# A two-layer diffusion backbone on one core: the first attention projection's weights are split beside the latents, and four pooling steps stand ahead of it

## The chip, the cores and the metric

The kernel runs on one core of one Trainium2 chip. The metric is the device time of one execution in microseconds (us), as the median of several runs. The core's engines each work through their own list of instructions in order: PE (TensorE, matrix products), DVE (VectorE), ACT (ScalarE), POOL (GpSimd) and SP (SyncE, which here only issues transfers from HBM).

## What is computed

Two layers over 256 latent tokens and 256 context tokens of width 2048; layer 0 is the one that the change touches. Cut to what matters:

```python
def even_mixer(hx, hc, w_in, q_norm, w_uq, kv_norm, w_ukv, w_pool, pool_scale, w_out, cos, sin, ctx_out):
    px = hx @ w_in                      # 512 query latents, 256 key/value latents, 64 rotary keys, 1024 pooling
    pc = hc @ w_in
    qn, qr = mla_queries(px, q_norm, w_uq)      # rmsnorm(query latents) @ w_uq, 8 heads
    kn, kr, v = mla_keys(px, kv_norm, w_ukv)    # rmsnorm(kv latents) @ w_ukv
    ckn, ckr, cv = mla_keys(pc, kv_norm, w_ukv)
    qr, kr = apply_rope(qr, cos, sin), apply_rope(kr, cos, sin)
    attn_x = latent_attention(qn, qr, concat(ckn, kn), concat(ckr, kr), concat(cv, v))
    pool_x = multiscale_pool(px[..., MLA_IN:], w_pool, pool_scale)   # 4 centred windows, then a 256x256 matrix each
    return concat(attn_x, pool_x) @ w_out
```

Around it stand adaptive norms (each scale and shift is a product of the conditioning vector with a 2048 x 2048 matrix), a squared-ReLU MLP of width 8192 in both layers, and a Fourier mixer in layer 1. All of it is float32.

## The kernel before

Activations lie transposed, features on partitions. A float32 product is made of three products of rounded halves: a weight tile `W` is loaded (`load`, 1 MB at most, six buffers), ACT rounds it into `H` (`split`, L135), DVE computes the rest `L = W - H` (L136), and PE multiplies H and L with the activations, H first. `H` and `L` have six buffers each. The second half of an activation is made in the same way (`split_pair`, `split_act`).

The adaptive vectors of layer 0 that the first stage doesn't need (`mod_vector`, 48 tiles of 1 MB) are not PE's work: DVE multiplies each tile with the conditioning vector and sums it, one SCALAR_TENSOR_TENSOR per tile (L103). `load` issues them: 1.75 of them for each weight tile in the mixer (`pace`), and all 48 must be summed before the norm that follows the mixer. They use the same six W buffers.

The mixer is two generators. `attention` squares the latents, makes their inverse norms (`var`, `rb`), scales them into kvh/kvl and ql, and then for each of four pairs of heads calls `project` (keys' part kn from w_ukv, the rotary query qr and the other query part qn from w_uq, values v), `scores` (with the softmax), `turned` (transposes of the probabilities) and `values`. `pooling` goes through the second half of the pooling input: four tiles of w_pl, each split in two halves, a step of 12 matmuls into `pu` for each half (steps 1 to 8 below; tiles 1 to 4), then `pl` (the windows, from the constants `band`), `po` (w_pool), and the pooled half of the output matrix w_oe. `weave` drives attention and, wherever it yields n, lets pooling take n steps. So the written order of the weave is the order of PE and of SP's transfers (both are in a manual schedule). The order of ACT and DVE is made by a scheduler when the kernel is built, and is fixed from then on.

Before the change, pooling takes one step after the squares, one after the first sums, and two after the latents; then `project(0)` loads and splits its two tiles. A blank step stands between step 8 and `pl`.

Of the kernel before, what the change touches and what calls it, by code (L numbers as in the profile page):

```python
# [43 lines left out]
def hybrid_dit(ctx: ExitStack, tc: tile.TileContext, xT, ctxT, c2, cb_in, vecs, wmod_s, wmod0, wmod1,  # L44
               w_kq, w_pl, w_uq, w_ukv, w_pool, w_oe, w_oo, w1, w2,
               rope, band, ident_in, sel_in, dftc, dftn, out):
    nc = tc.nc
# [14 lines left out]
    def funit(name="fu"):  # L62
        return ap.tile([P, 512], F32, name=name, tag="a")
# [13 lines left out]
    def half(b, i):  # L77
        return b[:, i * T:(i + 1) * T]
# [14 lines left out]
    def mod_step():  # L93
        l, which, norm, j, src = todo.pop(0)
        w = wp.tile([P, 2048], F32, name="W", tag="W")
        nc.sync.dma_start(w, src)
        late.append((w, l, which, norm, j))

    def mod_sums():

        while late:
            w, l, which, norm, j = late.pop(0)
            nc.vector.scalar_tensor_tensor(w, w, 1.0, cb, ALU.mult, ALU.mult,  # L103
                                           accum_out=mods[l][:, which, j:j + 1])
            if j == NB - 1:
                whole.add((l, which))
                v = mods[l][:, which]
                b = V_BM[l] + which * NB
                nc.vector.tensor_tensor(v, v, vec[:, b:b + NB], ALU.add)
                if norm is not None:  # L110
                    scales(mods[l], which, norm)
# [9 lines left out]
    def load(src, n=2048):  # L121
        mod_sums()
        w = wp.tile([P, 2048], F32, name="W", tag="W")
        nc.sync.dma_start(w[:, :n], src)
        pace[1] += pace[0]
        while pace[1] >= 1 and todo:
            pace[1] -= 1
            mod_step()
        return w

    def split(w, lo, n, nn):

        h = hp.tile([P, 1024], F32R, name="H", tag="H")
        l = hp.tile([P, 1024], F32R, name="L", tag="L")
        nc.scalar.copy(h[:, :n], w[:, lo:lo + n])  # L135
        nc.vector.tensor_tensor(l[:, :n], w[:, lo:lo + n], h.bitcast(F32)[:, :n], ALU.subtract)  # L136
        return [(h[:, i:i + nn], l[:, i:i + nn]) for i in range(0, n, nn)]

    def split_act(u, src, n=T):
        nc.scalar.copy(u[:, :n], src)  # L140
        nc.vector.tensor_tensor(u[:, n:2 * n], src, u.bitcast(F32)[:, :n], ALU.subtract)  # L141

    def split_pair(h, l, src):
        nc.scalar.copy(h, src)
        nc.vector.tensor_tensor(l, src, h.bitcast(F32), ALU.subtract)
# [195 lines left out]
    def column(i):  # L341
        return vec[:, i:i + 1]
# [153 lines left out]
    ropet = funit("ropet")  # L496
    nc.sync.dma_start(ropet.rearrange("p (a b) -> p a b", b=T), rope)
    bandt = [funit(f"band{i}") for i in range(4)]
    for i in range(4):
        nc.sync.dma_start(bandt[i], band[:, i])  # L500

    mod_vector(0, 2)
    mod_vector(0, 4, V_N2[0])
# [31 lines left out]
    def pooling():  # L535

        ut = [[funit("ut") for hf in range(2)] for tb in range(2)]
        for tb in range(2):
            nc.scalar.copy(ut[tb][0], pu0[tb])
        us = [bank(f"pu{tb}") for tb in range(2)]  # L540
        for kt in range(4):
            w = load(w_pl[1, kt])
            for i in range(2):
                for n, (h, l) in enumerate(split(w, 1024 * i, 1024, 512)):
                    by_token(us, 4 * kt + 2 * i + n, h, l)
                yield
        for tb in range(2):
            nc.scalar.copy(ut[tb][1], us[tb])
        yield
        pooled = []  # L550
        for g in range(4):
            ps = bank("pl")
            for j in range(2):
                fs = slice((g % 2) * T + j * P, (g % 2) * T + (j + 1) * P)
                for tb in range(2):
                    mm(half(ps, j), ut[tb][g // 2][:, fs], half(bandt[g], tb), j == 0 and tb == 0, j == 1 and tb == 1)
            pooled.append(funit("pl"))
            nc.scalar.copy(pooled[g], ps)
            if g % 2:
                yield  # L560
        w = load(w_pool)
        for g in range(4):
            ps = bank("po")
            for j in range(2):
                plain(half(ps, j), [w[:, k * 256:(k + 1) * 256] for k in (2 * g, 2 * g + 1)], j,
                      [half(pooled[g], 0), half(pooled[g], 1)], j == 0, j == 1)
            for j in range(2):
                u = unit("mx")
                sc, o = column(V_PS + 2 * g + j), half(ps, j)
                nc.scalar.mul(u[:, :T], o, sc)  # L570
                nc.vector.scalar_tensor_tensor(u[:, T:], o, sc, u.bitcast(F32)[:, :T], ALU.mult, ALU.subtract)
                mixed.append(u)
            if g % 2:
                yield
        for ng in range(4):
            yield from linear([((w_oe[ng, kt],), 4 * kt - 8) for kt in (2, 3)], mixed,
                              residual(0, 2, None, True)(ng), 4, True)
# [4 lines left out]
    def rotary(s):  # L582

        r = scr("rot")
        nc.vector.stream_shuffle(r, s, list(range(16, 32)) + list(range(16)))
        nc.vector.tensor_tensor(s, s, half(ropet, 0), ALU.mult)
        nc.vector.tensor_tensor(r, r, half(ropet, 1), ALU.mult)
        nc.vector.tensor_tensor(s, s, r, ALU.add)

    def attention():  # L590
        squares = []
        for b in ka[:2] + qa:
# [16 lines left out]
        for j in range(2):  # L609
            f = funit("kvf")  # L610
            nc.vector.scalar_tensor_tensor(f, ka[j], column(V_KN + j), rk, ALU.mult, ALU.mult)
            kvh.append(unit("kvh"))
            kvl.append(unit("kvl"))
            split_pair(kvh[j], kvl[j], f)
        for j in range(4):
            f = scr("ql")
            nc.vector.scalar_tensor_tensor(f, half(qa[j // 2], j % 2), column(V_QN + j), rq,
                                           ALU.mult, ALU.mult)
            ql.append(unit("qls"))
            split_act(ql[j], f)  # L620
        kr = funit("kr")
        nc.scalar.copy(kr, ka[2])
        rotary(half(kr, 1))
        krh, krl = unit("krh"), unit("krl")
        split_pair(krh, krl, kr)
        yield 2

        def project(pr):

            w = load(w_ukv[pr], 1024)  # L630
            wkv = split(w, 0, 1024, 512)
            kn, vt = [], []
            for j in range(2):
                js = slice(j * P, (j + 1) * P)
                ps = bank("kn")
                for k in range(2):
                    h, l = wkv[k]
                    mm(ps, h[:, js], kvh[k], k == 0, False)
                    mm(ps, h[:, js], kvl[k], False, False)
                    mm(ps, l[:, js], kvh[k], False, k == 1)  # L640
                kn.append((unit("knh"), unit("knl")))
                split_pair(*kn[j], ps)
            w = load(w_uq[pr], 1536)
            wuq = split(w, 0, 768, 384) + split(w, 768, 768, 384)
            ps = bank("qr")
            narrow(half(ps, 0), wuq, 2, ql, True, True)
            f = scr("qr")
            nc.scalar.copy(f, half(ps, 0))
            rotary(f)

            qr = (unit("qrh"), unit("qrl"))
            for j in range(2):
                nc.scalar.mul(half(qr[0], j), f, own[:, j:j + 1])
                nc.vector.scalar_tensor_tensor(half(qr[1], j), f, own[:, j:j + 1], half(qr[0], j).bitcast(F32),
                                               ALU.mult, ALU.subtract)
            ps = bank("qn")
            for j in range(2):
                narrow(half(ps, j), wuq, j, ql, j == 0, j == 1)
            qn = (unit("qnh"), unit("qnl"))
            split_pair(*qn, ps)  # L660
            for tb in range(2):
                ps = bank("v")
                for i in range(2):
                    ts = slice((2 * tb + i) * P, (2 * tb + i + 1) * P)
                    for k in range(2):
                        h, l = wkv[k]
                        mm(half(ps, i), kvh[k][:, ts], h[:, T:], k == 0 and i == 0, False)
                        mm(half(ps, i), kvl[k][:, ts], h[:, T:], False, False)
                        mm(half(ps, i), kvh[k][:, ts], l[:, T:], False, k == 1 and i == 1)
                vt.append(funit("v"))  # L670
                nc.scalar.copy(vt[tb], ps)
            return qn, qr, kn, vt
# [43 lines left out]
            attn.append(a)  # L716

        pair = project(0)
        yield 1
        p = scores((pair, 0))  # L720
        yield 2
# [272 lines left out]
```

## Time and profile before

| | us |
|---|---|
| median of 3 runs | 1979.73 |
| lowest, highest | 1978.56, 1980.13 |
| profiled execution, its own time | 1980.76 |
| its span in the trace | 1979.0 |
| PE busy / DVE busy / ACT busy | 1928.8 / 1455.6 / 1008.4 |
| mean busy share of the DMA engines by q1 | 72.9% |

A busy PE is not a PE at its peak: what counts is where it stands still and at what clock it runs. In the page's strip of 40 slices PE is at 90% or more in every slice but the first ones and the last; slice 4 of the granted clock reads 8 where nearly all others read 9. The places where PE waits are read from its instructions in order of time.

### The profile page before, as it was taken

Reading aid. Unit: us, or ns where it says so; the run is one execution under the profiler, and the core shown is the slowest. Engines: PE = TensorE matmul, PEld = TensorE weight load, DVE = VectorE, ACT = ScalarE, POOL = GpSimd, SP = SyncE. Lnnn points to the kernel's source line nnn. Section 1 sums busy time; section 2 is a strip of 40 time slices with the busy share of each in tenths; the row PEclk is TensorE's granted clock in tenths of the full one; section 3 lists DMA queues with packets and bytes.
Section 4 is the critical chain, followed back from the end, with each engine's and each line's share of the span. In section 5 each row is a group of like instructions: output and inputs, shape, how many; then the busy total and the mean of one; then the engine's idle time right before and its main releaser. Section 6 shows DMA issues by size and latency. Waiting matters only on the chain.

```text
span 1979.0 us, 29675 instructions
## 1 busy us (share of the span) xinstructions
PE 1928.8 (97%) x11886; PEld 1708.6 (86%) x11886; DVE 1455.6 (74%) x2042; ACT 1008.4 (51%) x1655; POOL 1.2 (0%) x13
## 2 busy tenths in 40 slices
PE   5998999999999999999999999999999999999997
PEld 4786899988888888888888989888888888888887
DVE  4548999998888888888888577897555555555564
ACT  3344654455545645554554454555455446544653
POOL 0000000000000000000000000000000000000000
PEclk9998999999999999999999999999999999999999
DMA  9997899879888888888998347597555555555541
GB/s 376 395 394 263 322 347 354 331 269 380 315 334 339 333 312 346 321 333 305 329 333 309 125 156 269 191 391 297 186 194 189 192 191 184 199 179 186 189 171 43
DMA packets 77466, 537.72 MB, mean 272 GB/s; under 512 B 8848, under 2 KB 9104, under 8 KB 14480
## 3 DMA queue, kind: packets, MB, share of 16 engines
q1 hardware_dynamic: 77328, 535.82, 72.9%
q8 instruction: 93, 1.52, 0.3%
q14 instruction: 45, 0.37, 0.1%
HBM read 533.69 MB, written 2.10 MB: 271 GB/s over the span
## 4 chain that ended last, share of the span: by engine, by line
PE 92%; DVE 5%; DMA 1%; issue 1%; ACT 1%; SPq 0%; DVEq 0%; ACTq 0%
PE mm L81 80%; PE ka L81 2%; DVE W L103 2%; PE mrow L81 1%; PE pu L81 1%; PE f L81 1%; PE qa L81 1%; DVE L L136 1%; PE sc L81 1%; DMA W<-in_wmod_s 1%; PE pv L81 1%; PE p L81 1%; PE var L81 0%; PE wk L81 0%; PE pl L81 0%
## 5 line engine op out<-in xcount | busy, mean ns | idle before, releaser
L136 DVE TENSOR_TENSOR L<-W,H 128x1024 fp32r<-128x1024 f32 (+1 forms) x620 | 736.3, 1213 | 266.2 <-ACT H L135 162.8
L135 ACT CAST H<-W 128x1024 fp32r<-128x1024 f32 (+1 forms) x620 | 628.8, 1042 | 526.6 <-PE mm L81 409.1
L81 PE MATMUL mm<-hid,H 128*128 128x512 f32 (+1 forms) x2176 | 509.8, 378 | 0.0
L81 PE MATMUL mm<-h,H 128*128 128x512 f32 x2048 | 495.1, 391 | 0.0
L81 PEld LDWEIGHTS mm<-hid,H 128*128 128x128 f32 x2176 | 390.9, 189 | 66.6
L81 PEld LDWEIGHTS mm<-h,H 128*128 128x128 f32 x2048 | 374.3, 188 | 72.0 <-DVE h L302 1.0
L103 DVE SCALAR_TENSOR_TENSOR W<-W,cb 128x2048 f32<-128x2048 f32 x160 | 364.7, 2283 | 0.2 <-DMA W<-in_wmod 0.2
L81 PE MATMUL mm<-hid,L 128*128 128x256 f32 x2048 | 290.0, 283 | 0.0
L81 PEld LDWEIGHTS mm<-hid,L 128*128 128x128 f32 x2048 | 274.7, 191 | 11.7
L81 PEld LDWEIGHTS mm<-h,L 128*128 128x128 f32 x2048 | 266.8, 191 | 12.5
L81 PE MATMUL mm<-h,L 128*128 128x256 f32 x2048 | 270.6, 283 | 0.0
L522 DVE SCALAR_TENSOR_TENSOR x<-mm,mods,x 128x256 f32<-128x256 f32 x176 | 81.2, 479 | 90.0 <-ACT rt L521 72.7
L758 DVE TENSOR_TENSOR g<-mm,b 128x256 f32<-128x256 f32 x128 | 53.7, 420 | 49.4 <-ACT b L757 48.6
L521 ACT ACTIVATE rt<-mm,mods 128x256 f32<-128x256 f32 x132 | 58.8, 470 | 61.0 <-PE mm L81 60.9
L757 ACT COPY b<-mm 128x256 f32<-128x256 f32 x128 | 45.8, 358 | 64.5 <-PE mm L81 64.5
L760 ACT ACTIVATE rl<-g 128x256 f32<-128x256 f32 x128 | 53.4, 417 | 47.2 <-DVE g L758 45.8
L81 PE MATMUL mm<-fr,H 128*128 128x512 f32 (+1 forms) x320 | 69.5, 348 | 0.0
L81 PEld LDWEIGHTS mm<-fr,H 128*128 128x128 f32 x320 | 55.1, 190 | 6.7
L761 ACT ACTIVATE hd<-rl 128x256 f32<-128x256 f32 x128 | 53.3, 417 | 3.0
L141 DVE TENSOR_TENSOR hid<-hd,hid 128x256 fp32r<-128x256 f32 x128 | 53.6, 419 | 0.5 <-ACT hid L140 0.5
L524 DVE TENSOR_TENSOR x<-x,rt 128x256 f32<-128x256 f32 x132 | 52.4, 418 | 1.1
L140 ACT CAST hid<-hd 128x256 fp32r<-128x256 f32 x128 | 52.2, 408 | 1.0
(224 smaller groups left out, 1558.8 us busy)
## 6 DMA issues: line engine op xcount, KB each, us to landing
W<-in_w SPq DMA_DIRECT2D x256, 1024.0 KB, 4.9
W<-in_wmod SPq DMA_DIRECT2D x160, 1024.0 KB, 6.1
W<-in_wmod_s SPq DMA_DIRECT2D x32, 1024.0 KB, 9.7
W<-in_w_oe SPq DMA_DIRECT2D x16, 1024.0 KB, 6.9
W<-in_w_oo SPq DMA_DIRECT2D x16, 1024.0 KB, 4.9
W<-in_w_pl SPq DMA_DIRECT2D x8, 1024.0 KB, 8.8
W<-in_w_kq SPq DMA_DIRECT2D x8, 896.0 KB, 9.4
W<-in_w_uq SPq DMA_DIRECT2D x4, 768.0 KB, 4.6
```

The source lines that it names most:

```text
L81: nc.tensor.matmul(o, l, r, start=start, stop=stop, skip_group_check=True)
L103: nc.vector.scalar_tensor_tensor(w, w, 1.0, cb, ALU.mult, ALU.mult, accum_out=mods[l][:, which, j:j + 1])
L135: nc.scalar.copy(h[:, :n], w[:, lo:lo + n])
L136: nc.vector.tensor_tensor(l[:, :n], w[:, lo:lo + n], h.bitcast(F32)[:, :n], ALU.subtract)
L140: nc.scalar.copy(u[:, :n], src)
L141: nc.vector.tensor_tensor(u[:, n:2 * n], src, u.bitcast(F32)[:, :n], ALU.subtract)
L521: nc.scalar.mul(t, half(ps, 1), g)
L522: nc.vector.scalar_tensor_tensor(x[:, i], ps[:, :T], g, x[:, i], ALU.mult, ALU.add)
L524: nc.vector.tensor_tensor(x[:, i], x[:, i], t, ALU.add)
L758: nc.vector.tensor_tensor(s, half(ps, 0), b, ALU.add)
L760: nc.scalar.activation(r, s, AF.Relu)
L761: nc.scalar.square(f, r)
```

## The change

`project(0)` no longer loads its weights itself. Its w_ukv tile is loaded and split when the key latents are scaled, its w_uq tile when the query latents are (`ready`); later pairs load as before. Attention yields 4 instead of 2 ahead of `project(0)`, so pooling steps 3 to 6 stand there instead of 3 and 4. The rotation of the keys' rotary part, and its split, are written behind `project(0)`. The four loads of the band constants, which stood ahead of the mixer, follow the weights of pooling tiles 1 to 4 one by one. The blank pooling step is gone.

```diff
-    for i in range(4):
-        nc.sync.dma_start(bandt[i], band[:, i])
@@ pooling()
                     by_token(us, 4 * kt + 2 * i + n, h, l)
                 yield
+            nc.sync.dma_start(bandt[kt], band[:, kt])
         for tb in range(2):
             nc.scalar.copy(ut[tb][1], us[tb])
-        yield
         pooled = []
@@
+    def key_weights(pr):
+        return split(load(w_ukv[pr], 1024), 0, 1024, 512)
+
+    def query_weights(pr):
+        w = load(w_uq[pr], 1536)
+        return split(w, 0, 768, 384) + split(w, 768, 768, 384)
@@ attention()
             split_pair(kvh[j], kvl[j], f)
+        ready = [key_weights(0)]
         for j in range(4):
@@
             split_act(ql[j], f)
+        ready.append(query_weights(0))
         kr = funit("kr")
         nc.scalar.copy(kr, ka[2])
-        rotary(half(kr, 1))
         krh, krl = unit("krh"), unit("krl")
-        split_pair(krh, krl, kr)
-        yield 2
+        yield 4
         def project(pr):
-            w = load(w_ukv[pr], 1024)
-            wkv = split(w, 0, 1024, 512)
+            wkv = ready.pop(0) if ready else key_weights(pr)
@@
-            w = load(w_uq[pr], 1536)
-            wuq = split(w, 0, 768, 384) + split(w, 768, 768, 384)
+            wuq = ready.pop(0) if ready else query_weights(pr)
@@
         pair = project(0)
+        rotary(half(kr, 1))
+        split_pair(krh, krl, kr)
         yield 1
```

DVE's list right behind the norm of the latents, before. The first row is the second half of pooling tile 2 (for step 4), the last one w_ukv of pair 0; kvf, kvl, ql and qls are the scaled latents and their splits:

```order
L136 TENSOR_TENSOR L<-W,H 128x1024
L611 SCALAR_TENSOR_TENSOR kvf<-ka_113,vec,rk 128x512
L617 SCALAR_TENSOR_TENSOR ql<-qa_111,vec,rq 128x256 x2
L617 SCALAR_TENSOR_TENSOR ql<-qa_112,vec,rq 128x256
L145 TENSOR_TENSOR kvl<-kvf,kvh 128x512
L611 SCALAR_TENSOR_TENSOR kvf<-ka_114,vec,rk 128x512
L617 SCALAR_TENSOR_TENSOR ql<-qa_112,vec,rq 128x256
L103 SCALAR_TENSOR_TENSOR W,mods_102<-W,cb 128x2048
L145 TENSOR_TENSOR kvl<-kvf,kvh 128x512
L141 TENSOR_TENSOR qls<-ql,qls 128x256 x4
L585 STREAM_SHUFFLE rot<-kr 128x256
L136 TENSOR_TENSOR L<-W,H 128x1024
```

The same place in the changed kernel, where 128x768 is w_uq of pair 0 (w_ukv's split stands ahead of the norm), and the last row is pooling tile 2 with both halves, for steps 3 and 4:

```order
L616 SCALAR_TENSOR_TENSOR kvf<-ka_113,vec,rk 128x512
L136 TENSOR_TENSOR L<-W,H 128x768
L145 TENSOR_TENSOR kvl<-kvf,kvh 128x512
L616 SCALAR_TENSOR_TENSOR kvf<-ka_114,vec,rk 128x512
L623 SCALAR_TENSOR_TENSOR ql<-qa_111,vec,rq 128x256 x2
L145 TENSOR_TENSOR kvl<-kvf,kvh 128x512
L141 TENSOR_TENSOR qls<-ql,qls 128x256 x2
L623 SCALAR_TENSOR_TENSOR ql<-qa_112,vec,rq 128x256 x2
L103 SCALAR_TENSOR_TENSOR W,mods_102<-W,cb 128x2048
L141 TENSOR_TENSOR qls<-ql,qls 128x256 x2
L103 SCALAR_TENSOR_TENSOR W,mods_102<-W,cb 128x2048
L136 TENSOR_TENSOR L<-W,H 128x1024 x2
```

The split of pooling tile 2 has moved from ahead of the latents to behind all of them and behind two vector sums. In PE's list pooling steps 3 to 6 follow the norm's `rb` products directly, as steps 3 and 4 did.

DVE's list at the end of `project(0)` and through the first softmax, before. The 128x1024 rows are the two halves of pooling tile 4, and then w_ukv of pair 1:

```order
L145 TENSOR_TENSOR qnl<-qn,qnh 128x512
L136 TENSOR_TENSOR L<-W,H 128x1024
L685 TENSOR_REDUCE mx<-sc 128x1
L136 TENSOR_TENSOR L<-W,H 128x1024
L686 TENSOR_SCALAR mx<-mx 128x1
L685 TENSOR_REDUCE mx<-sc 128x1
L103 SCALAR_TENSOR_TENSOR W,mods_102<-W,cb 128x2048
L689 RECIPROCAL rc<-sm 128x1
L686 TENSOR_SCALAR mx<-mx 128x1
L103 SCALAR_TENSOR_TENSOR W,mods_102<-W,cb 128x2048
L689 RECIPROCAL rc<-sm 128x1
L136 TENSOR_TENSOR L<-W,H 128x1024
```

The same place now, where the 128x1024 row is again pooling tile 4:

```order
L145 TENSOR_TENSOR qnl<-qn,qnh 128x512
L145 TENSOR_TENSOR krl<-kr,krh 128x512
L136 TENSOR_TENSOR L<-W,H 128x1024 x2
L103 SCALAR_TENSOR_TENSOR W,mods_102<-W,cb 128x2048 x2
L688 TENSOR_REDUCE mx<-sc 128x1 x2
L689 TENSOR_SCALAR mx<-mx 128x1 x2
L692 RECIPROCAL rc<-sm 128x1 x2
L688 TENSOR_REDUCE mx<-sc 128x1
L689 TENSOR_SCALAR mx<-mx 128x1
L688 TENSOR_REDUCE mx<-sc 128x1
L692 RECIPROCAL rc<-sm 128x1
L689 TENSOR_SCALAR mx<-mx 128x1
```

Tile 4 has moved behind the split of the rotary keys (krl), and no vector sum stands between the rows of the softmaxes of heads 0 and 1.

DVE's list at `project(1)` now, where 128x1024 is w_ukv and 128x768 w_uq of pair 1 and `mx<-po` are pooled outputs:

```order
L692 RECIPROCAL rc<-sm 128x1
L103 SCALAR_TENSOR_TENSOR W,mods_102<-W,cb 128x2048
L141 TENSOR_TENSOR at<-pv,at 128x256
L103 SCALAR_TENSOR_TENSOR W,mods_102<-W,cb 128x2048
L569 SCALAR_TENSOR_TENSOR mx<-po,vec,mx 128x256
L136 TENSOR_TENSOR L<-W,H 128x1024
L569 SCALAR_TENSOR_TENSOR mx<-po,vec,mx 128x256 x2
L103 SCALAR_TENSOR_TENSOR W,mods_102<-W,cb 128x2048
L569 SCALAR_TENSOR_TENSOR mx<-po,vec,mx 128x256
L145 TENSOR_TENSOR knl<-kn,knh 128x512 x2
L103 SCALAR_TENSOR_TENSOR W,mods_102<-W,cb 128x2048
L136 TENSOR_TENSOR L<-W,H 128x768 x2
```

Before, at the same place, w_uq of pair 1 (128x768) stood between the rows of head 1's softmax, ahead of knl of pair 1:

```order
L136 TENSOR_TENSOR L<-W,H 128x768
L689 RECIPROCAL rc<-sm 128x1
L686 TENSOR_SCALAR mx<-mx 128x1
L136 TENSOR_TENSOR L<-W,H 128x768
L103 SCALAR_TENSOR_TENSOR W,mods_102<-W,cb 128x2048
L689 RECIPROCAL rc<-sm 128x1
L141 TENSOR_TENSOR at<-pv,at 128x256
L103 SCALAR_TENSOR_TENSOR W,mods_102<-W,cb 128x2048
L145 TENSOR_TENSOR knl<-kn,knh 128x512
L103 SCALAR_TENSOR_TENSOR W,mods_102<-W,cb 128x2048
L145 TENSOR_TENSOR knl<-kn,knh 128x512
```

The split of w_uq for pair 1 has moved from inside that softmax to behind four vector sums, the split of w_ukv and knl.

## Rows read from the trace of the kernel before

**Rows 1.** the page, part 1: busy time of each engine

```profile
PE 1928.8 (97%) x11886; PEld 1708.6 (86%) x11886; DVE 1455.6 (74%) x2042; ACT 1008.4 (51%) x1655; POOL 1.2 (0%) x13
```

**Rows 2.** windows: each engine busy us (instructions), granted clock, DMA share, GB/s

```profile
core 0: us, PE busy (x) PEld busy (x) DVE busy (x) ACT busy (x) POOL busy (x), PEclk, DMA share, GB/s
...
170.00:180.00 10.00, 5.16 (x18) 3.64 (x16) 10.00 (x16) 4.51 (x9) 0.00 (x0) 0.81 0.70 238
180.00:190.00 10.00, 7.12 (x46) 7.12 (x47) 10.00 (x16) 3.97 (x5) 0.00 (x0) 0.67 0.96 370
...
260.00:300.00 40.00, 38.61 (x276) 36.10 (x275) 39.25 (x58) 21.69 (x36) 0.00 (x0) 1.00 0.93 342
300.00:340.00 40.00, 39.10 (x285) 36.93 (x285) 38.32 (x56) 20.11 (x33) 0.00 (x0) 1.00 0.95 351
340.00:400.00 60.00, 58.17 (x448) 55.92 (x446) 55.89 (x82) 26.54 (x39) 0.00 (x0) 0.97 0.89 341
```

**Rows 3.** PE in order of time (start, us, line, output<-inputs, [idle <-releaser]): where it waited

```profile
174.78 0.50 PE L81 MATMUL kn<-kvh,L 128*128 128x512 f32 x1 [3.46 <-DVE L L136]
...
182.88 0.58 PE L81 MATMUL qr<-qls,L 128*128 128x256 f32 x1 [4.26 <-DVE L L136]
...
195.39 0.50 PE L81 MATMUL sc<-knh,qnl 128*128 128x512 f32 x1 [0.50 <-DVE qnl L145]
...
204.53 0.98 PE L701 MATMUL tr<-ident,p 128*128 128x128 f32 x7 [1.01 <-ACT p L690]
...
215.48 0.99 PE L701 MATMUL tr<-ident,p 128*128 128x128 f32 x7 [2.65 <-ACT p L690]
```

**Rows 4.** PE in order of time: pooling steps, half clock, project(1), windows, scores, values

```profile
165.15 0.48 PE L81 MATMUL pu<-H,h 128*128 128x512 f32 x1
...
170.71 0.39 PE L81 MATMUL kn<-kvh,H 128*128 128x512 f32 x1
...
176.70 0.63 PE L81 MATMUL kn<-kvh,H 128*128 128x512 f32 x1
177.13 0.63 PE L81 MATMUL kn<-kvl,H 128*128 128x512 f32 x1
...
191.53 0.40 PE L81 MATMUL pu<-H,h 128*128 128x512 f32 x1
...
216.22 0.48 PE L81 MATMUL kn<-kvh,H 128*128 128x512 f32 x1
...
226.23 3.62 PE L81 MATMUL pl<-band,ut 128*128 128x256 f32 x16
229.50 0.58 PE L81 MATMUL sc<-knh,qnh 128*128 128x512 f32 x1
...
232.45 1.89 PE L81 MATMUL pv<-pu,v 128*128 128x256 f32 x8
```

**Rows 5.** DVE in order of time, behind the norm of the latents

```profile
163.24 1.22 DVE L136 TENSOR_TENSOR L<-W,H 128x1024 fp32r<-128x1024 f32 x1
164.67 0.75 DVE L611 SCALAR_TENSOR_TENSOR kvf<-ka,vec,rk 128x512 f32<-128x512 f32 x1 [0.20 <-ACT rk L606]
165.90 1.27 DVE L617 SCALAR_TENSOR_TENSOR ql<-qa,vec,rq 128x256 f32<-128x256 f32 x3 [0.48 <-ACT rq L607]
...
171.83 1.42 DVE L141 TENSOR_TENSOR qls<-ql,qls 128x256 fp32r<-128x256 f32 x4
...
175.32 2.28 DVE L103 SCALAR_TENSOR_TENSOR W<-W,cb 128x2048 f32<-128x2048 f32 x1
...
181.88 1.81 DVE L136 TENSOR_TENSOR L<-W,H 128x768 fp32r<-128x768 f32 x2
```

**Rows 6.** DVE in order of time: its longest wait ahead of the norm

```profile
148.96 2.36 DVE L136 TENSOR_TENSOR L<-W,H 128x1024 fp32r<-128x1024 f32 x2 [7.38 <-ACT H L135]
```

**Rows 7.** ACT in order of time: one rounding, last row of the first softmax

```profile
165.76 1.05 ACT L135 CAST H<-W 128x1024 fp32r<-128x1024 f32 x1
...
203.76 0.72 ACT L690 ACTIVATE p<-p,rc 128x512 f32<-128x512 f32 x1 [0.94 <-DVE rc L689]
```

## The prediction

> **What bounds the kernel now.** I read the page's busy times first: PE is busy for 97% of the span and DVE for 74% [rows 1], an average over stages with different limits. So the second view is the table of windows at the place that the change touches. There PE does not keep its 97%: it is busy for 5.16 of the ten us from 170 and 7.12 of the ten from 180, at a granted clock of 0.81 and 0.67, while DVE is busy for the whole of both windows [rows 2]. From 260 to 400 both are nearly full: PE stands still for 1.4, 0.9 and 1.8 us, DVE for 0.75, 1.7 and 4.1 [rows 2]. Third I read PE's instructions in order of time for what ended its waits: 3.46 us ahead of the first product with L of w_ukv, 4.26 us ahead of the first with L of w_uq, both released by DVE's split; then 0.50 us for qnl, 1.01 and 2.65 us for the probabilities of heads 0 and 1 [rows 3]. All of it is 11.9 us of idle PE. Behind the two long waits PE ran at its lower level, 1.2 of 2.4 GHz: kn products start 0.43 us apart [rows 4], where the pooling steps' 24 products take 5.56 us from 165.15 to 170.71, or 0.23 each [rows 4]. Some five kn products, the qr triples and two qn triples were so slow; at 0.2 us a product of 512 columns and half of that for 256 this is about 2.6 us. So at most 14.5 us can be had here, 10.3 of it at the two splits that the change moves. DVE is the engine that ends the waits, and it works through its list strictly as built. The question is therefore what now stands ahead in that list of what PE needs next.
>
> **Part 1: w_ukv and w_uq are split early.** Both splits are ahead of the latents' last rows in the new list, and PE needs them later. The two waits of 3.46 and 4.26 go: -7.7 us, and with them the 2.6 us of half clock.
>
> **Part 2: pooling tile 2 is split late.** PE's list has steps 3 to 6 directly behind the norm's products, at 165.15 [rows 4]. Before, tile 2's second split ran at 163.24 [rows 5], in time. Now the list holds, from 163.24 on and ahead of the first half of tile 2: two halves of w_uq (1.75 us by the row at 181.88), two kvf (0.75 each by the row at 164.67, less overlap 1.35), two kvl (1.25), four ql (1.7, by the three in 1.27), four qls (1.4), two vector sums (2.2 each, 4.4) and the half itself (1.15) [rows 5]. That is 13.0 us; with waits for rk, rq and kvh as in these rows (0.2 and 0.48, and one more of that size) 13.8. So L of step 3 is there at 177.0, and PE can do one product with H in the meantime: a new wait of 11.6 us. Behind it stand the other half of tile 2 (1.15), two more sums (4.4) and the first half of tile 3 (1.15), so step 5 can start at 183.7. PE's 23 remaining products of steps 3 and 4 take 5.3 us at full clock and would end at 182.3, so it waits 1.4 more, or runs slow in that time, which comes to the same; with all 23 at the half clock they would end at 186.9, and that is the upper bound. Steps 5 and 6 (5.56) end at 189.2, `project(0)` takes 10.0 us by pair 1, which ran undisturbed from 216.22 to 226.23 [rows 4], and ends at 199.2. Before, it ended at 191.53 with steps 5 and 6 still to do [rows 4], so the same work stood at 197.1. The sum of parts 1 and 2 is +2.1 us, with +5.3 as the upper bound.
>
> **Part 3: rotary keys behind project(0).** The seven rows that rotate and split them cost DVE the same as before. But in the new lists ACT rounds tile 4 behind the copies of v and of the rotary keys, and DVE splits it behind krl. Step 7 is PE's next work after `project(0)`. After the last product of v come a copy and a rounding of 512 (0.6 each, as the 0.57 to 0.75 us of 512-wide rows), a rounding of 1024 (1.05) [rows 7] and the split (1.21) [rows 5]: 3.4 us, less one product with H: +3.2 us of wait, nothing as the lower bound if v's copy were early. The 0.50 us for qnl [rows 3] goes, since step 7 and the split of qnl come before: -0.5. Running sum +4.8.
>
> **Part 4: the first softmaxes.** The blank step is gone, and no vector sum stands between the softmax rows. Step 8 and the first `pl` (2.78 + 3.27) [rows 4] cover the first softmax, which took from the end of the scores at 197.8 to the probabilities at 204.5 [rows 7] and is now shorter, though two sums stand ahead of it. For head 1 `pl` and `po` (twice 3.27) come between. The waits of 1.01 and 2.65 [rows 3] go: -3.7. Running sum +1.1.
>
> **Part 5: w_uq of pair 1.** It now stands behind the last reciprocal of head 1 and, in this order, two sums (4.4), a split of `at` (0.4), four pooled outputs (0.45 each, 1.7), w_ukv (1.15), another sum (2.2), two knl (1.25), another sum (2.2) and its own first half (0.87): 14.2 us by [rows 5], and the reciprocal comes some 2.7 us behind the scores (the maximum, the exponential and their handing over, each 0.7 [rows 7]). In these 16.9 us PE has values (1.7), `pl` and `po` (6.5), transposes (0.8) and kn (2.8): 11.8. So it waits about 4.8 us ahead of qr of pair 1, where before it did not wait at all: the kn at 216.22 went straight on. Less a pair with H: +4.6. Running sum +5.7.
>
> **Part 6: the clock behind the new waits.** The two waits of before were each followed by 1.0 to 1.6 us of loss at the lower level [rows 4]. The two new ones, of 3.2 and 4.6 us, are of that size: +2.7, with 0 and +4 as bounds. Sum +8.4.
>
> **Edits at nothing.** The band transfers only change places among transfers, 1 MB in all; nothing reads them for 70 us. w_ukv and w_uq are issued earlier, and no wait here ends with a transfer. If one did, it would cost its landing, 5 to 9 us. DVE does the same work, but idles more: about 9 us more in the softmaxes, 4 during steps 5, 6 and kn, 3 ahead of krl, and less ahead of the norm, where 5.4 of the 7.38 us [rows 6] go, since ACT now rounds tile 1 ahead of the squares. That is some 13 us net of DVE work pushed back. I take nothing for it in the sum, since from 260 on DVE too stands still now and then, for 6.5 us in all [rows 2], and so has something to catch up with, but keep up to +5 as a bound.
>
> The profiled execution took 1980.76 us, 1.0 above the median. 1980.76 + 8.4 is 1989.2 for an execution like it, and 1988.1 for a median: **1988 us**.
>
> **Rivals.** (a) *The change does what its shape suggests*: two waits and the half clock go, and nothing comes. For it: both waits in [rows 3] are ended by just the two splits that now come earlier. Against it: what PE needs first behind the norm is no longer in front in DVE's list. It needs tile 2 split by 165, 12 us sooner than I work out. Time: 1979.7 - 10.3 = 1969. This is where a rule of the Trainium skill (Perfetto Trace Analysis, section Optimization Strategy) leads: find the gaps on the engine that should be full, find what ends them, and make that start sooner. The trace agrees on the gaps, but the rule alone says nothing of what is pushed back on the engine that ends them. Chance 0.08. (b) *The later losses don't come*: parts 1 to 4 hold (+1.1), yet w_uq of pair 1 is in time, because DVE gets out of the softmax earlier than I think, and the clock stays up. Time about 1981 to 1982. For it: the waits of part 5 hang on 2.7 us that I pieced together. Chance 0.13. (c) *DVE can't catch up*: all 48 sums must be done ahead of the norm behind the mixer, and from 260 to 400 DVE has only 6.5 us left [rows 2], part of it where it waits for PE. Then DVE's 13 us decide, not PE's 8.4: 1993 to 1994. It decides if a split of w_oe comes later than PE's products ask for it. Chance 0.18. (d) The forecast, 1984 to 1991: 0.58. What is left, 0.03, lies outside of all.
>
> **How the numbers follow.** About 0.2%, 4 us, is what a measurement of this kernel can tell from no change. Slower by more is the forecast, (c) and a little of (b): 0.80. Within: nearly all of (b): 0.12. Faster: (a): 0.08. The range leaves out (a), the lower edge of (b) and the outer part of (c): 1981 to 1995.
>
> **What would show it.** Right: PE waits some 11 us behind the `rb` products and is released by a split of tile 2; waits of 3 us ahead of step 7 and 5 us ahead of qr of pair 1, both released by L136; no waits for probabilities of heads 0 and 1; DVE idle in the first softmaxes. Wrong: if tile 2's split starts before 170, part 2 falls and (a) is near; if PE keeps its lateness but the end of the mixer moves by more than 10 us, (c); if a transfer ends one of the waits, the working above misses it.

## The result, and the profile after

| | us |
|---|---|
| median before, same chip | 1979.93 (1978.56 to 1981.56) |
| median after | 2000.18 (1995.01 to 2000.97) |
| ratio, 95% interval | 1.0096 (1.0083 to 1.0108) |
| profiled execution after, its span | 2000.97, 1999.2 |

The change costs 20 us. The direction was forecast, the size was not: 1988, with a range of 1981 to 1995. One of the four runs after took 1995.0, the other three 1999.6 to 2001.0, and no run here tells why.

The page's busy times after, beside [rows 1]. PE's 11886 products are the same and take 7.2 us more; the span grew by 20.2, so PE stands still for 13.0 us more. DVE's work is the same within 1.2 us, so it idles for 19 us of the difference.

```profile
PE 1936.0 (97%) x11886; PEld 1714.9 (86%) x11886; DVE 1456.8 (73%) x2042; ACT 1007.1 (50%) x1655; POOL 1.2 (0%) x13
```

PE in order of time, after, where it waited or ran slow behind a wait (start, us, line, output<-inputs, [idle <-releaser]); these answer to [rows 3]:

```profile
172.36 0.80 PE L81 MATMUL pu<-H,h 128*128 128x512 f32 x1 [7.18 <-ACT H L135]
176.72 0.79 PE L81 MATMUL pu<-L,h 128*128 128x512 f32 x1 [3.56 <-DVE L L136]
177.31 1.05 PE L81 MATMUL pu<-H,h 128*128 128x512 f32 x2
178.16 0.63 PE L81 MATMUL pu<-L,h 128*128 128x512 f32 x1
...
190.22 0.39 PE L81 MATMUL kn<-kvh,H 128*128 128x512 f32 x1
...
202.43 0.50 PE L81 MATMUL pu<-H,h 128*128 128x512 f32 x1 [2.14 <-ACT H L135]
203.69 0.80 PE L81 MATMUL pu<-L,h 128*128 128x512 f32 x1 [0.76 <-DVE L L136]
...
235.55 0.50 PE L81 MATMUL qr<-qls,H 128*128 128x256 f32 x2 [1.41 <-ACT H L135]
239.23 0.58 PE L81 MATMUL qr<-qls,L 128*128 128x256 f32 x1 [3.18 <-DVE L L136]
...
373.80 0.58 PE L81 MATMUL mm<-at,L 128*128 128x256 f32 x1 [2.01 <-DVE L L136]
...
381.69 0.39 PE L81 MATMUL mm<-at,L 128*128 128x256 f32 x1 [0.42 <-DVE L L136]
...
390.50 0.39 PE L81 MATMUL mm<-at,L 128*128 128x256 f32 x1 [2.76 <-DVE L L136]
...
398.29 0.50 PE L81 MATMUL mm<-at,H 128*128 128x256 f32 x2 [0.53 <-ACT H L135]
...
400.19 0.39 PE L81 MATMUL mm<-at,L 128*128 128x256 f32 x1 [1.40 <-DVE L L136]
```

The waits of [rows 3] are gone. In their place stand the three that were forecast (10.7 us for pooling tile 2, 2.9 ahead of step 7, and 4.6 ahead of qr of pair 1), each in two parts, for H and for L. At the end of the mixer stand waits for H and L of w_oe, 7.1 us in all; before, they were 1.2:

```profile
378.49 0.39 PE L81 MATMUL mm<-at,L 128*128 128x256 f32 x1 [0.42 <-DVE L L136]
...
385.10 0.39 PE L81 MATMUL mm<-at,L 128*128 128x256 f32 x1 [0.55 <-DVE L L136]
...
386.32 0.39 PE L81 MATMUL mm<-at,L 128*128 128x256 f32 x1 [0.25 <-DVE L L136]
```

Counted from PE's rows as time less the products done at full speed, PE has lost some 10 us more than in the kernel before by 250 and 11 by 370. The norm behind the mixer starts 21 us later (its first product at 413.19 against 391.99). So half of the loss arises at the early waits and half at w_oe.

Why DVE idles is told by SP. First what SP waited for from 130 to 260 in the kernel after (engine and line, releaser, us in total, times, longest), then its issues in order of time:

```profile
SPq L124 <- DVE L L136: 33.7, 7, 15.0
...
SPq L124 <- DVE at L141: 17.2, 1, 17.2
SPq L545 <- PE pu L81: 12.8, 2, 10.5
```

```profile
172.67 0.33 SPq L96 DMA_DIRECT2D W<-in_wmod  x1
183.61 0.33 SPq L545 DMA_DIRECT2D band<-in_band  x1
184.03 0.38 SPq L124 DMA_DIRECT2D W<-in_w_pl  x1
...
188.12 0.39 SPq L124 DMA_DIRECT2D W<-in_w_pool  x1
188.60 0.88 SPq L96 DMA_DIRECT2D W<-in_wmod  x2
204.80 0.33 SPq L124 DMA_DIRECT2D W<-in_w_ukv  x1
207.01 2.54 SPq L96 DMA_DIRECT2D W<-in_wmod  x2
226.54 0.33 SPq L124 DMA_DIRECT2D W<-in_w_uq  x1
```

L545 is the band load. SP stands 10.5 us in front of the third one, until a product of pooling step 4 ends, and behind it in SP's list stand w_pl of tile 4, the fourth band, w_pool and their vector tiles. Tile 4 then comes late, is split late, and w_ukv of pair 1 waits 15.0 us for the W buffer that this split frees; w_uq of pair 1 waits 17.2. From 190 to 229 SP issues four transfers. In the windows (as in [rows 2]: PE, PEld, DVE, ACT, POOL busy, clock, DMA share, GB/s) that is 225 GB/s and a DVE busy for 38.55 of 60 us, first after, then before:

```profile
180.00:240.00 60.00, 52.52 (x250) 44.24 (x249) 38.55 (x60) 25.01 (x45) 0.00 (x0) 0.90 0.62 225
```

```profile
180.00:240.00 60.00, 52.96 (x289) 46.56 (x290) 56.63 (x83) 30.77 (x56) 0.00 (x0) 0.95 0.87 336
```

DVE lacks what it would have done in the gaps, the vector sums: from 180 to 240 it does 8 of them, before 14. By 260 it has done 18 of the 48, before 23, and by 340 35 against 40. So five sums, 11 us of DVE's work, are still owed when w_oe begins. Its two longest waits from 180 to 240, after:

```profile
192.40 0.69 DVE L145 TENSOR_TENSOR knl<-kn,knh 128x512 fp32r<-128x512 f32 x1 [5.70 <-ACT knh L144]
...
220.55 0.69 DVE L688 TENSOR_REDUCE mx<-sc 128x1 f32<-128x512 f32 x1 [6.00 <-PE sc L81]
```

### The profile page after: what moved, and what is told of

It reads as the page before. It is cut to its first block, busy times and chain, and to the rows that moved or that the text cites. A ratio compares the mean times of both kernels' runs of the same rounds, so it can differ in the third digit from the quotient of the medians.

```text
span 1999.2 us, 29656 instructions
## 1 busy us (share of the span) xinstructions
PE 1936.0 (97%) x11886; PEld 1714.9 (86%) x11886; DVE 1456.8 (73%) x2042; ACT 1007.1 (50%) x1655; POOL 1.2 (0%) x13
## 4 chain that ended last, share of the span: by engine, by line
PE 92%; DVE 4%; DMA 1%; issue 1%; ACT 1%; SPq 0%; DVEq 0%; ACTq 0%
PE mm L81 79%; PE pu L81 2%; PE ka L81 2%; PE mrow L81 2%; DVE L L136 1%; PE f L81 1%; PE qa L81 1%; PE sc L81 1%; DVE W L103 1%; DMA W<-in_wmod_s 1%; PE p L81 1%; PE pv L81 1%; PE qn L81 0%; PE v L81 0%; DVE x L520 0%
## 5 line engine op out<-in xcount | busy, mean ns | idle before, releaser
L81 PE MATMUL pu<-H,h 128*128 128x512 f32 x128 | 46.4, 433 | 9.3 <-ACT H L135 9.3
L251 ACT ACTIVATE q<-x 128x256 f32<-128x256 f32 x52 | 21.5, 417 | 63.1 <-DVE x L520 46.2
```

The source lines that it names most:

```text
L81: nc.tensor.matmul(o, l, r, start=start, stop=stop, skip_group_check=True)
L251: nc.scalar.square(q, src)
```

## The experiments

Theory 1 was the forecast's: what costs time is the place of each split in DVE's list. Theory 2: the two more steps ahead of `project(0)`. Theory 3, formed from SP's rows after the first four runs: the band loads hold up SP's queue. Ratios are to the kernel before on the same chip, with 95% intervals.

### Two steps instead of four

```diff
-        yield 4
+        yield 2
```

> The changed kernel with two pooling steps ahead of project(0) instead of four; w_ukv and w_uq of pair 0 stay early, tile 2 of pooling stays split behind the latents and two vector sums. Theory 1 (the place of tile 2's split in DVE's list costs the time): the wait of 10.7 us behind the rb products stays whole, project(0) then goes straight through, tile 3 is split during it, and steps 5 and 6 find it ready; the waits of 2.9 us ahead of step 7 and of 4.6 us ahead of qr of pair 1 shrink or go, since tile 4 comes later and w_uq of pair 1 has fewer sums ahead of it. 1990 to 1996 us. Theory 2 (the fourth and third extra steps cost the time, because they put project(0) and all DVE work behind it 5.6 us later): most of the 20 us is gone, 1978 to 1984.

Measured: 2001.1 us, 1.0104 (1.009 to 1.0118), as slow as the change itself. Theory 2 falls by this run. Theory 1 misses too: it has the long wait right, but the 4 to 10 us that it saw come back didn't come. SP's waits in this run, from 130 to 260, pointed to what both had left out, long waits in front of band loads, one of them until the split of the rotary keys (krl):

```profile
SPq L545 <- PE pu L81: 28.4, 2, 20.5
...
SPq L545 <- DVE krl L145: 13.6, 1, 13.6
```

### Four steps alone

The kernel before, with only:

```diff
-        yield 2
+        yield 4
```

> The kernel before with only the four pooling steps ahead of project(0); both weight tiles of pair 0 are loaded and split after them, tile 2 of pooling stays ahead of the latents in DVE's list. Theory 1: no wait behind the rb products, steps 3 and 4 run from 165 to 171; then tile 3 (its split stands where w_ukv's did) costs a wait of about 3.5 us, w_ukv one of about 3 and w_uq one of about 3.5, 10 us against the 7.7 of before, while steps 7, 8 cover more of the softmax: 1978 to 1986. Theory 2 (the four steps themselves cost it): 1990 to 2000, with PE late at the end of the mixer by 10 us or more.

Measured: 1981.2 us, 1.0007 (0.9998 to 1.0016). Waits of 3.39 us for tile 3 (expected 3.5) and 3.68 for w_uq (3.5) take the place of the two long ones in [rows 3]; the one for w_ukv (3) didn't come. The waits for the probabilities of heads 0 and 1 grew, to 2.58 and 3.74 us, where they were expected to be covered better. All in all the four steps cost nothing that can be told from no change.

### Pooling tile 2 split ahead of the norm

The changed kernel, with both tiles loaded and split at once:

```diff
-            w = load(w_pl[1, kt])
+            if kt == 0:
+                w0, w1_ = load(w_pl[1, 0]), load(w_pl[1, 1])
+                halves = [split(w0, 0, 1024, 512), split(w0, 1024, 1024, 512)]
+                ahead = [split(w1_, 0, 1024, 512), split(w1_, 1024, 1024, 512)]
+            elif kt == 1:
+                halves = ahead
```

> The changed kernel, but pooling tile 2 is loaded right behind tile 1 and split ahead of the norm; the rest as in the changed kernel, four steps ahead of project(0). In DVE's list tile 3 now stands behind the latents, both halves of w_uq and three to four sums, ready at about 182. Theory 1: the wait behind rb goes, steps 3 and 4 run from 165 to 171, and a wait of the same size, 9 to 11 us, comes ahead of step 5, released by tile 3's split; the rest as in the changed kernel: 1996 to 2001, nothing gained, since it is the place in a full list and not one tile that decides. If only tile 2's place mattered: 1986 to 1990.

Measured: 1996.8 us, 1.0078 (1.0065 to 1.0091). The wait moved as expected, from step 3 to step 5 (1.31 and 7.63 us, 8.9 in all), and little was gained, some 3 us. That fits theory 1, but since SP stood 7.4 us at a band load here too, it doesn't tell it from theory 3.

### The same with two steps

As above, and `yield 2`.

> As the kernel with pooling tile 2 split ahead of the norm, and with two steps ahead of project(0): the list of DVE then serves PE in the order in which PE asks (tile 2, w_ukv, w_uq, tile 3). Theory 1: no long wait behind rb; kn of pair 0 starts at 171; w_uq, behind the latents and two sums, is ready at about 176 against kn's end at 173.5, a wait of 2 to 3 us; steps 5 and 6 find tile 3 split. Of the 7.7 us of waits some 5 go, and part of that is given back at the end of the mixer, since DVE idles as long as before: 1974 to 1981. Theory 2 (early weights push DVE work back whatever the order): 1985 or more.

Measured: 1991.1 us, 1.0053 (1.0039 to 1.0066). No wait behind `rb` is left and PE is busy for 39 of the 40 us from 140 to 180; the wait for w_uq didn't come, and one of 4.3 us came ahead of step 5, where none was expected. Still 11 us are lost. This is where theory 1 fell: PE had what it asked for first, in its order. Theory 2, as put for this run, still held. What remained in SP's rows was again a band load (here L554), now for 14.3 us:

```profile
SPq L554 <- PE pu L81: 17.7, 2, 9.4
...
SPq L554 <- DVE krl L145: 14.3, 1, 14.3
```

### The bands ahead of the mixer again

The changed kernel, with this part alone undone:

```diff
+    for i in range(4):
+        nc.sync.dma_start(bandt[i], band[:, i])
@@ pooling()
-            nc.sync.dma_start(bandt[kt], band[:, kt])
```

> The changed kernel with the four band loads back ahead of the mixer; weights early, four steps, rotary keys late and no blank step stay. Theory 3 (SP's queue: in the trace of the changed kernel SP stands 10.5 us ahead of a band load, whose buffer a pooling step still reads, and all weights and vector tiles behind it come late, so that DVE runs out of sums in the softmaxes and idles 21 us from 180 to 240): the band's stall goes, tile 4 and the weights of pair 1 come some 10 us sooner, DVE idles less than 10 us from 180 to 240, and the waits for L of w_oe at 374 to 390 go; the wait of 10 us for tile 2 stays: 1983 to 1989. Theory 1 (only the order of DVE's splits counts, bands cost nothing): 1998 to 2002.

Measured: 1981.1 us, 1.0002 (0.9993 to 1.001). All of the loss is gone, with the weights early and four steps ahead: theory 3, if 2 us better than it had it, and nothing is left for theory 2. PE's waits and the window of this kernel:

```profile
172.18 0.80 PE L81 MATMUL pu<-H,h 128*128 128x512 f32 x1 [7.19 <-ACT H L135]
178.90 0.79 PE L81 MATMUL pu<-L,h 128*128 128x512 f32 x1 [5.92 <-DVE L L136]
...
191.74 0.39 PE L81 MATMUL kn<-kvh,H 128*128 128x512 f32 x1
...
206.59 0.50 PE L81 MATMUL sc<-krl,qrh 128*128 128x512 f32 x1 [1.12 <-DVE krl L145]
```

```profile
180.00:240.00 60.00, 58.88 (x320) 51.39 (x319) 54.14 (x80) 31.71 (x56) 0.00 (x0) 0.97 0.84 313
```

The wait for tile 2 is longer than after the change (13.1 against 10.7 us) and `project(0)` starts later (191.74 against 190.22), yet the kernel is 19 us faster. DVE is busy for 16 us more from 180 to 240. The waits ahead of step 7 and of qr of pair 1 are gone, and so are those for w_oe: they had been consequences of the late loads.

### The bands alone

The kernel before, with the band loads between the pooling weights and no blank step (the band lines of the change, and `-        yield`).

> The kernel before with the band loads between the pooling weights and without the blank step, nothing else. Theory 3: SP stalls at a band load behind a pooling step here too, DVE idles 10 us more from 180 to 240 and PE gets waits of 4 to 8 us and loses some more at the end of the mixer: 1984 to 1995. Theory 1 (bands and blank step cost nothing): 1978 to 1981.

Measured: 2003.9 us, 1.0118 (1.0104 to 1.0132): the two edits that the prediction costed at nothing lose 23 us, more than the whole change, and more than theory 3 had worked out. The blank step is not it: the kernel with the bands ahead lacks it too. SP's row, from 130 to 260:

```profile
SPq L545 <- PE pu L81: 47.2, 2, 28.0
```

### Rotary keys ahead again

The changed kernel, with the rotation and `split_pair(krh, krl, kr)` back ahead of the yield.

> The changed kernel with the rotation and split of the rotary keys back ahead of project(0). Tile 4 no longer stands behind krl: the wait of 2.9 us ahead of step 7 goes or shrinks to 1. SP waits 15.0 us for the buffer that tile 4's split frees, and could be 1 to 3 us sooner. Theory 1 (each displaced split costs its own wait): 1996 to 1998. Theory 3 (SP's stall at the band load sets when tile 4 is there at all): 1998 to 2001, nothing gained, since tile 4's load is issued at 184 either way.

Measured: 1999.6 us, 1.0093 (1.0077 to 1.0108), nothing gained. The wait ahead of step 7, expected to go or to shrink to 1 us, is 2.4 against 2.9, and the one behind `rb` has grown from 10.7 to 14.0: the lists of ACT and DVE are built anew for each kernel.

### Shorter sums, in both kernels

```diff
-            w, l, which, norm, j = late.pop(0)
-            nc.vector.scalar_tensor_tensor(w, w, 1.0, cb, ALU.mult, ALU.mult,
+            w, l, which, norm, j = late.pop(0); m = 256 if (l, which) == (0, 3) and 4 <= j < 10 else D
+            nc.vector.scalar_tensor_tensor(w[:, :m], w[:, :m], 1.0, cb[:, :m], ALU.mult, ALU.mult,
```

> The changed kernel, but six of the 48 vector sums, those that DVE does from about 324 to 352 us, read 256 of their 2048 columns, so that DVE has some 11 us less to do there (the six columns of that vector are then not what the reference asks). If DVE's lateness sets the end of the mixer: the waits of 5.2 us for L of w_oe at 374 to 391 and the half clock behind them go, 1991 to 1995. If these waits come from late transfers or from the clock alone: 1998 to 2001.

> The kernel before with the same six vector sums on 256 of 2048 columns (six columns of that vector are then not what the reference asks), as a control for the changed kernel, which gained 4.2 us by it. If DVE's lateness belongs to the change: 0 to 2 us here (the kernel before waits 1.6 us for L of w_oe and sums at its mixer's end): 1978 to 1981. If DVE bounds the mixer in either kernel: 4 us or more, 1974 to 1977.

Measured: the changed kernel 1996.0, 1.0077 (1.0064 to 1.0089); the kernel before 1979.9, 0.9998 (0.9989 to 1.0007). In the kernel before, 11 us less of DVE's work are worth nothing; in the changed kernel they are worth some 4 us, as far as can be told: 4.2 us is less than the 5 to 9 expected, and the interval overlaps that of the change. Of the waits for w_oe only the first, of 2.0 us, is gone; left are these, and 0.5 and 1.4 us at the last tile:

```profile
376.01 0.39 PE L81 MATMUL mm<-at,L 128*128 128x256 f32 x1 [0.42 <-DVE L L136]
...
384.83 0.39 PE L81 MATMUL mm<-at,L 128*128 128x256 f32 x1 [2.75 <-DVE L L136]
```

What ends the longest that is left can be read from the changed kernel's ACT and DVE, ahead of PE's row at 390.50:

```profile
383.44 1.98 ACT L135 CAST H<-W 128x1024 fp32r<-128x1024 f32 x2
...
384.81 2.28 DVE L103 SCALAR_TENSOR_TENSOR W<-W,cb 128x2048 f32<-128x2048 f32 x1
...
387.02 2.28 DVE L103 SCALAR_TENSOR_TENSOR W<-W,cb 128x2048 f32<-128x2048 f32 x1
...
389.24 2.35 DVE L136 TENSOR_TENSOR L<-W,H 128x1024 fp32r<-128x1024 f32 x2
```

The tile has landed and is rounded by 385.4, and DVE, without a gap, does two vector sums before it splits it. So this wait is not for a transfer: it is for sums that stand ahead of the split in DVE's list. In the run with shorter sums those two are at full length, and the wait stays. The wait that went, at 373.80 in the changed kernel, also has two sums ahead of its split (367.44 and 369.98), and those two are among the six that were shortened.

### The bands at the same place, from POOL

```diff
-            nc.sync.dma_start(bandt[kt], band[:, kt])
+            nc.gpsimd.dma_start(bandt[kt], band[:, kt])
```

> The changed kernel, with the four band loads at the same place of the program but issued by POOL instead of SP. Same transfers, same buffers, same waits of each transfer for the pooling step that frees its buffer; only what stands behind that wait on SP is free. Theory 3 (SP's queue stands behind the waiting band load): 1979 to 1983, like the kernel with the bands ahead; DVE idles some 18 us from 140 to 260 as there, no 10 us stall of SP at a pooling load. Rival (the band transfers themselves, or their buffers taken at another time, cost it): 1995 to 2001.

Measured: 1979.3 us, 0.9996 (0.9987 to 1.0005). The same four transfers stand at the same place of the program, and three of them again wait for pooling products of PE, now on an engine with nothing else to do. POOL's issues, and SP's, in order of time:

```profile
152.50 0.54 POOL L545 DMA_DIRECT2D band<-in_band  x1 [6.16 <-PE pu L81]
182.83 0.54 POOL L545 DMA_DIRECT2D band<-in_band  x1 [29.80 <-PE pu L81]
```

```profile
174.52 0.33 SPq L124 DMA_DIRECT2D W<-in_w_pl  x1
...
189.01 0.33 SPq L124 DMA_DIRECT2D W<-in_w_ukv  x1
...
203.41 0.33 SPq L124 DMA_DIRECT2D W<-in_w_uq  x1
```

The third band is issued at 182.83 against 183.61, hardly sooner than from SP, but tile 4's weights go out 9.5 us earlier, and those of pair 1 by 15.8 and 23.1. This settles it for theory 3: it is neither the transfers nor the waits for their buffers, but what stands behind those waits on SP. Since the lists of ACT and DVE are built anew, that includes the list which the scheduler built around the stall; how much of the 20 us is the stall itself and how much that list, no run separates. The Trainium skill states where such a wait is spent (DMA: Bandwidth & Descriptors, section Anatomy of one DMA — SWDGE (gpsimd) path): "any semaphore wait happens on the issuing sequencer before dispatch". The two traces agree, with 10.5 us of SP's time, and 29.8 of POOL's, in front of the third load.

### In PE's order, bands ahead

Tile 2 split ahead of the norm, two steps, and the band loads ahead of the mixer.

> The kernel with tile 2 of pooling split ahead of the norm and two steps ahead of project(0) (1991.1 us with the bands between), with the bands ahead of the mixer. Theory 3: SP's stalls of 14.3 and 17.7 us at band loads go. What PE asks for behind the norm is then split in its order: no wait of 13 us behind rb as with the bands ahead in the changed kernel; one of 2 to 4 us for w_uq; of the 14.5 us that the kernel before loses here and in the first softmaxes 5 to 9 come back: 1971 to 1977. Rival (the list of DVE is full from 165 to 260 whatever its order, and the waits only move): 1979 to 1983.

Measured: 1976.4 us, 0.9977 (0.9969 to 0.9986), faster than both kernels. Two short waits are left where the kernel before lost 7.7 us:

```profile
176.68 0.58 PE L81 MATMUL qr<-qls,L 128*128 128x256 f32 x1 [3.50 <-DVE L L136]
...
188.39 0.50 PE L81 MATMUL pu<-L,h 128*128 128x512 f32 x1 [3.02 <-DVE L L136]
```

In the first softmaxes 0.3 us is left of 4.2. The change is worth 4 us in this form, with SP's queue free and tile 2 at its place. How the 4 us divide among the early weights, the blank step and the late rotary keys, this run doesn't separate; by the waits, more of it lies in the softmaxes than at the weights.

### Products in the long wait

The kernel with the bands ahead, and in the wait behind `rb`:

```diff
+        awake(hx * 4, 54)
```

> The changed kernel with the bands ahead of the mixer (1981.1 us), with 54 products of 512 columns more behind rb, whose result nobody reads, so that PE works through most of its wait of 13.1 us there. If the half clock behind that wait costs time: pooling steps 3 and 4 run at 0.23 us a product instead of some 0.4, worth 1 to 3 us: 1978 to 1980. If tile 3's split sets steps 5 and 6 anyway: no gain, 1980 to 1982.

Measured: 1980.1 us, 1.0001 (0.9992 to 1.001). The granted clock from 170 to 190 rises from 0.50 and 0.83 to 1.00 and the pooling steps run at full speed, but no gain can be told from none:

```profile
170.00:180.00 10.00, 9.41 (x42) 7.45 (x42) 10.00 (x14) 4.66 (x8) 0.00 (x0) 1.00 0.53 194
180.00:190.00 10.00, 9.04 (x40) 7.15 (x39) 10.00 (x10) 3.14 (x3) 0.00 (x0) 1.00 1.00 388
```

PE then waits for tile 3, which it had not done before, and kn of pair 0 starts at 191.48 against 191.74:

```profile
186.12 0.50 PE L81 MATMUL pu<-L,h 128*128 128x512 f32 x1 [0.96 <-DVE L L136]
```

## Why the prediction was right and wrong

- **Part 1** held: kn of pair 0 follows step 6 without a wait, and qr follows kn.
- **Part 2** held: L of step 3 was forecast for 177.0 and came for 176.72, the wait was 10.7 us against 11.6, and kn of pair 0 began at 190.22 against 189.2.
- **Parts 3 and 5** had the right sizes (2.9 us against 3.2, 4.6 against 4.6; part 5's own terms, 16.9 less 11.8, give 5.1 and not 4.8, so 4.9 in all) but not the right cause. I took them for the price of moving the rotary keys and the weights. The list that I read them from had been made, when the kernel was built, around band loads that hold up the rest. With the bands ahead of the mixer and the keys still late, both are gone. Undoing the move of the keys gained nothing.
- **Part 4** held: no wait for the probabilities of heads 0 and 1.
- **Part 6**, the clock, was too small in its own terms: behind the 10.7 us PE's products start 0.43 us apart until 182.4, some 13 of the 24 of steps 3 and 4, and again behind the waits for w_oe. I had counted 2.7 us, and at steps 3 and 4 1.4 as wait or slow clock, more only as an upper bound; PE's busy time grew by 7.2. Filling the long wait, in the kernel with the bands ahead, gained nothing; the slow stretches behind the waits for w_oe were not tested.
- **Edits at nothing** is the step that failed. It said of the bands: "The band transfers only change places among transfers, 1 MB in all; nothing reads them for 70 us." That asks when a transfer lands and who reads it. It doesn't ask what the load itself waits for, nor what is queued behind it on SP. The band buffers come from the same pool (`funit`, `unit`) as the pooling input, and a load between two pooling tiles waits, by SP's rows, for a pooling step's products. Priced at 0, the edit is worth 23 us alone (with the blank step) and all of the 20 us here. I should have put the four loads down as a wait on SP, with the weights and sums of the next 50 us behind it. The sign that I named for such a miss, a transfer that ends one of PE's waits, didn't show: the wait is SP's, and PE's rows name the split that came late by it.
- **The DVE term**, taken at nothing with +5 as its bound, followed from the same miss. I counted 13 us more idling from DVE's list (my own terms, 9, 4 and 3 less 5.4, give 10.6); the windows show 18 in the 60 us from 180 alone, because the sums that would have filled the gaps were issued late or stood behind late splits in the list. DVE never caught up: it owed five sums at 260, and at 340 still.
- **The rivals.** (c) named the place where the loss grows, the splits of w_oe behind a DVE that can't catch up, and the sums that DVE still owes there bear out that part; its price of 13 us was short, and its cause, DVE's list alone, left out SP. (b)'s sum for parts 1 to 4, +1.1, is about what the change gives without the band loads: +0.2 by the medians, -1.4 to +2.0 by the interval. None of the four had SP as its mechanism. That the change came out slower, as forecast, is luck: without the edit priced at nothing it can't be told from no change.

## What to carry to other kernels

A load is not free because its data is small and wanted late: on an engine that only issues transfers, ask what each one waits for before it can go, and what stands behind it. Buffers from a shared pool turn a load's place in the program into a wait for the buffer's last reader. Where such a load has to stand there, issue it from a queue that nothing urgent shares.

A wait of 13 us on the busiest engine can be cheaper than a starved feeder, here DVE, which makes what PE multiplies: the kernel with the longer wait was the faster by 19 us, because DVE stayed supplied. And a list made at build time already holds the consequences of a stall, so waits read from it can be sized right and blamed on the wrong edit.

## What was not expected

Full clock behind the long wait was worth nothing that can be told: 1980.1 us against 1981.1, with intervals that overlap, though some 13 products there took about 0.2 us less each. What came next, steps 5 and 6, was set by DVE's split of tile 3.
